# Interleaving the latents' output projection and second norm with the context's layer-1 projections, on split PSUM banks

## The chip, the cores and the metric

The kernel runs on one core of a Trainium2 chip. The metric is the device time of one execution in microseconds (us), median of several runs. The engines are TensorE (PE, matmul), VectorE (DVE), ScalarE (ACT), GpSimd (POOL) and SyncE (SP, which issues most DMAs). PSUM, where matmuls accumulate, is used as eight banks of 128 x 512 fp32 values.

## What is computed

A backbone of two layers reads 512 latent tokens (`lat`) and 256 context tokens (`ctx`), width 1024, both through the same weights. Cut to what matters here, with `x` either stream:

```python
for l in range(DEPTH):                               # DEPTH = 2
    h  = modulate(rmsnorm(x, norm1[l]), ...)         # per-token rms, per-channel scale and shift
    y  = mixers(h @ w_in[l])                         # delta rule, windowed attention, HGRN2
    x  = x + m2 * (y @ w_out[l])                     # output projection, gated residual
    x  = x + m5 * sqrelu_mlp(modulate(rmsnorm(x, norm2[l]), ...), w_ff1[l], w_ff2[l])
return rmsnorm(x_lat, norm_f)
```

The context reads only itself; the latents read context and latents. In the last layer the context is needed only as far as the mixers' keys, values and states, so its layer-1 work is a norm, part of `w_in`, and two recurrences. It has no output projection and no MLP there.

## The kernel before

Activations lie transposed, channels on the 128 partitions, as eight tiles `x[k]` of 128 x T. A product of fp32 precision is made of three matmuls on split operands: high weight times high activation, high times low, low times high (L554, L555 and L556 in `product_t`). `product_t` takes one 128 x 1024 weight piece and makes one 128 x T output in a bank of kind "d": 24 matmuls. `product_n` (L572 to L574) makes the context's or latents' `abvi` outputs token-major, 128 x 400 for each block of 128 tokens (a "cell", two for the context), in banks of kind "dn", over four pieces of two channel tiles each.

Each piece is loaded by SP (L538), rounded to its high half by ACT (the CAST of L540) and its low half is made by DVE (L541). Staging, high and low halves each have a ring of two slots, so a piece's CAST waits until the matmuls of the piece two before it have ended.

A norm has three parts. `rstd` squares the eight tiles on ACT (L627), adds them on DVE (L628), sums over channels with tiny matmuls (L631), takes a Newton inverse root with twelve small DVE instructions (L634, L515 to L520), builds diagonal tiles (L638) and broadcasts the result with a matmul into a bank `pb` (L640). `modulated` then makes, for each of eight tiles, a scaled copy from `pb` (DVE L650), its high half (ACT L653) and its low half (DVE L654). The squares, the scaled copies, the spilled gates and the MLP's temporaries all take their 128 x 512 buffers from one ring of two, `ev`.

PSUM banks are handed out by kind, round robin: "d" has banks 0 and 1, "dn" 0, 1, 3, 4, 5 and 6, "n" 4 to 7.

The order on each engine comes from a scheduler that places the instructions by priority, which is the order in which the Python code emits them; weight pieces are emitted at a raised priority. `run` emits several generators side by side: each yields an estimated number of us, and the one that is furthest behind, after division by its speed, goes next.

Around the change the program is: the context's layer-0 output projection and MLP end; `project(1, (ctx,))` makes the context's layer-1 norm; `out_proj(0, lat)` runs eight products `m0` to `m7` of 512 columns, each evacuated by L1472 onto `x[m]`; the first step of `mlp(0, lat)` makes the latents' norm; `context_in` runs the context's layer-1 projections (`abvi`, then the delta keys and values `k0`, `k1`, `v0`, `v1` with a convolution after each, then the gates `hf00` to `hf11`, whose results are spilled to DRAM by POOL, then `sk`); then the latents' MLP (`ff1`, `ff2`) runs with the context's recurrences beside it.

Of the kernel before, what the change touches and what calls it, by code (L numbers as in the profile page):

```python
# [273 lines left out]
def run(*streams):  # L274

    at = [[0.0, i, g, speed] for i, (g, speed) in enumerate((x if isinstance(x, tuple) else (x, 1.0)) for x in streams)]
    while at:
        a = min(at)
        try:
            a[0] += next(a[2]) / a[3]  # L280
        except StopIteration:
            at.remove(a)
# [22 lines left out]
class Net:  # L305
# [334 lines left out]
        nc.tensor.matmul(pb, lhsT=self.c["ones"], rhs=dg, start=True, stop=True)  # L640
        return pb

    def modulated(self, l, which, seg, pb=None):
        nc = self.nc
        if pb is None:
            pb = self.rstd(seg)
        h = self.split(seg)
        for k in range(8):
            t = self.ev(seg.T)
            nc.vector.scalar_tensor_tensor(out=t, in0=seg.x[k], scalar=self.gmul[l][:, which, k, seg.idx:seg.idx + 1], in1=pb,  # L650
                                           op0=ALU.mult, op1=ALU.mult)
            sh = self.mod(l, 3 * which, k, seg)
            nc.scalar.activation(out=h.hi(k), in_=t, func=AF.Identity, bias=sh)  # L653
            nc.vector.scalar_tensor_tensor(out=h.lo(k), in0=t, scalar=sh, in1=h.hi(k).bitcast(F32), op0=ALU.add, op1=ALU.subtract)  # L654
        return h


    def in_piece(self, l, name):
# [27 lines left out]
    def project(self, l, segs):  # L686

        for seg in segs:
            if seg.x is None:
                self.x_load(seg)  # L690
        pbs = [self.rstd(seg, "n") for seg in segs]
        if l == 0:
            ring = Ring(self, 8, 1024)
            run(self.ada(0, 0, ring))
            ring.free()
        for seg, pb in zip(segs, pbs):
            seg.h = self.modulated(l, 0, seg, pb)
            self.x_free(seg)
            seg.r, seg.b, seg.need = {}, {}, seg is self.lat or l < DEPTH - 1
            if seg is self.ctx:  # L700
                seg.kv0 = l * 256
# [771 lines left out]
            yield from self.product_t(self.io["wout"][l, m][:, ks[0] * 128:(ks[-1] + 1) * 128], [(seg, h)], evac, len(ks))  # L1473
        h.free()

    def mlp(self, l, seg):
        nc = self.nc
        h = self.modulated(l, 1, seg)
        yield 0.0
        f = self.split(seg)  # L1480
        for g in range(4):
            for k in range(8):
                def evac(seg, ps):
                    t = self.ev(seg.T)
                    nc.scalar.activation(out=t, in_=ps, func=AF.Relu)  # L1485
                    nc.scalar.activation(out=t, in_=t, func=AF.Square)  # L1486
                    nc.scalar.copy(f.hi(k), t)  # L1487
                    nc.vector.tensor_tensor(out=f.lo(k), in0=t, in1=f.hi(k).bitcast(F32), op=ALU.subtract)  # L1488
                yield from self.product_t(self.io["ff1"][l, g * 8 + k], [(seg, h)], evac)
            for m in range(8):  # L1490
                def evac(seg, ps):
                    nc.vector.scalar_tensor_tensor(out=seg.x[m], in0=ps, scalar=self.mod(l, 5, m, seg), in1=seg.x[m], op0=ALU.mult, op1=ALU.add)  # L1492
                yield from self.product_t(self.io["ff2"][l, g, m], [(seg, f)], evac)
        h.free()
        f.free()
# [16 lines left out]
    def run(self, stop=None):  # L1512
        self.setup()
        lat, ctx = self.lat, self.ctx
# [40 lines left out]
        def context_in():  # L1555
            self.reserve((ctx,), "dk", "dv")
            yield from self.project_dn(1, (ctx,))
            yield from self.project_hg(1, (ctx,))
            yield from self.project_swa(1, (ctx,))
            ctx.h.free()  # L1560
# [12 lines left out]
        self.region_type(F32R, "r2", "r3")  # L1573
        run(bg.rest())
        self.project(1, (ctx,))
        run(self.out_proj(0, lat))
        mlp = self.mlp(0, lat)
        next(mlp)
        run(context_in())
        Ub = self.delta_open((ctx,))  # L1580

        def context():
# [4 lines left out]
            yield from self.hgrn(1, ctx, False)  # L1587

        run(self.ahead(context(), 3000), mlp)
        self.x_store(lat)  # L1590
        self.main = False
# [70 lines left out]
```

## Time and profile before

| | us |
|---|---|
| median of 3 runs | 2117.33 (2115.97 to 2119.23) |
| profiled execution | 2116.83 |
| span of its trace | 2115.0 |
| PE busy in the span | 1977.7 (94%) |
| DVE busy | 1219.3 (58%) |
| ACT busy | 857.6 (41%) |

A busy time is the sum of an engine's instructions in one profiled execution; lines like L554 are lines of the kernel before. The granted clock is the clock of TensorE that the throttle granted, as a share of full speed: 1.00 is 2.4 GHz and 0.50 is 1.2 GHz. Matmul durations overlap, so the distance from start to start tells the rate.

### The profile page before, as it was taken

How to read it: one execution, taken by the hardware profiler on the slowest of the kernel's cores; microseconds unless marked ns; L12 is line 12 of the kernel's file. 1: busy time of each engine (PE TensorE's matmuls, PEld its weight loads, DVE VectorE, ACT ScalarE, POOL GpSimd, SP SyncE). 2: the span in 40 equal slices, each digit the busy share in tenths (PEclk: the TensorE clock that was granted, in tenths of full speed). 3: DMA queues.
4: the chain of work that ended last, by engine and by line, in shares of the span. 5: the costliest groups of instructions: out<-in, count | busy, mean ns of one | idle time of the engine just before them, and what ended most of it. 6: DMA issues, size and time to landing. Idle time of an engine off the chain costs nothing.

```text
span 2115.0 us, 37910 instructions
## 1 busy us (share of the span) xinstructions
PE 1977.7 (94%) x15456; PEld 1620.8 (77%) x15456; DVE 1219.3 (58%) x2737; ACT 857.6 (41%) x1703; POOL 144.2 (7%) x281
## 2 busy tenths in 40 slices
PE   5999998799999999699999998999899979999996
PEld 2787887688899898588888876767678747888885
DVE  4574856666976667577333334666887483333334
ACT  2432353235465564353434242324555234334241
POOL 0001231200000000010000000011200000000000
PEclk9999999799999999899999999999999999999998
DMA  8435342145233243243222235464300222222221
GB/s 336 156 111 165 93 130 77 57 163 188 95 111 106 100 147 111 85 151 105 95 100 94 96 113 187 140 186 154 122 20 2 81 70 91 99 98 92 100 90 70
DMA packets 72445, 242.43 MB, mean 115 GB/s; under 512 B 10192, under 2 KB 12368, under 8 KB 72144
## 3 DMA queue, kind: packets, MB, share of 16 engines
q1 hardware_dynamic: 57456, 197.35, 27.7%
q0 software_dynamic: 11792, 34.14, 5.1%
q10 hardware_dynamic: 3024, 8.53, 1.2%
q8 instruction: 121, 1.98, 0.4%
q14 instruction: 52, 0.43, 0.1%
HBM read 218.21 MB, written 19.14 MB: 112 GB/s over the span
## 4 chain that ended last, share of the span: by engine, by line
PE 78%; DVE 9%; DMA 6%; issue 4%; ACT 2%; POOL 1%; ACTq 0%; DVEq 0%; POOLq 0%
PE psum L554 20%; PE psum L556 19%; PE psum L555 19%; PE psum L590 2%; PE psum L1444 2%; DMA arena<-in_ada 1%; PE psum L1435 1%; PE psum L1382 1%; DVE weights L541 1%; PE psum L1109 1%; PE psum L1067 1%; PE psum L1261 1%; DMA arena<-in_ff 1%; PE psum L1071 1%; DVE arena L1272 1%
## 5 line engine op out<-in xcount | busy, mean ns | idle before, releaser
L554 PE MATMUL psum<-r,weights 128*128 128x512 f32 (+1 forms) x2304 | 830.4, 361 | 11.7 <-ACT arena L725 4.2
L556 PE MATMUL psum<-r,weights 128*128 128x512 f32 (+1 forms) x2304 | 826.6, 360 | 2.1 <-DVE weights L541 2.0
L555 PE MATMUL psum<-r,weights 128*128 128x512 f32 (+1 forms) x2304 | 825.0, 359 | 1.3 <-DVE r L1464 1.0
L540 ACT CAST weights<-arena 128x1024 fp32r<-128x1024 f32 (+3 forms) x295 | 293.3, 995 | 700.1 <-PE psum L555 600.4
L541 DVE TENSOR_TENSOR weights<-arena,weights 128x1024 fp32r<-128x1024 f32 (+3 forms) x295 | 340.5, 1155 | 294.6 <-ACT weights L540 286.4
L554 PEld LDWEIGHTS psum<-r,weights 128*128 128x128 f32 x2304 | 435.9, 189 | 96.1 <-issue 9.6
L556 PEld LDWEIGHTS psum<-r,weights 128*128 128x128 f32 x2304 | 435.8, 189 | 74.2 <-DVE weights L541 6.3
L555 PEld LDWEIGHTS psum<-r,weights 128*128 128x128 f32 x2304 | 435.8, 189 | 70.1 <-issue 3.9
L1492 DVE SCALAR_TENSOR_TENSOR arena<-psum,arena 128x512 f32<-128x512 f32 (+1 forms) x96 | 63.3, 660 | 200.6 <-PE psum L556 200.4
L1488 DVE TENSOR_TENSOR r<-arena,r 128x512 fp32r<-128x512 f32 (+1 forms) x96 | 57.5, 601 | 35.2 <-ACT r L1487 34.8
L653 ACT ACTIVATE r<-arena 128x512 fp32r<-128x512 f32 (+1 forms) x56 | 33.1, 627 | 71.0 <-DVE arena L650 71.0
L590 PE MATMUL psum<-arena 128*32 128x256 f32 x576 | 53.1, 416 | 9.0 <-DMA arena<-in_ada 8.3
L1382 PE MATMUL psum<-r 128*128 128x256 f32 (+1 forms) x256 | 53.6, 320 | 1.7 <-ACT r L1415 1.3
L1486 ACT ACTIVATE arena<-arena 128x512 f32<-128x512 f32 (+1 forms) x96 | 54.0, 564 | 2.4
L1487 ACT CAST r<-arena 128x512 fp32r<-128x512 f32 (+1 forms) x96 | 52.5, 551 | 2.7 <-ACT arena L1428 0.3
L1485 ACT ACTIVATE arena<-psum 128x512 f32<-128x512 f32 (+1 forms) x96 | 50.2, 523 | 0.0
L1472 DVE SCALAR_TENSOR_TENSOR arena<-psum,arena 128x512 f32<-128x512 f32 (+1 forms) x40 | 27.6, 694 | 33.9 <-PE psum L556 33.8
L572 PE MATMUL psum<-weights,r 128*128 128x400 f32 x96 | 35.4, 382 | 10.7 <-DVE arena L650 10.1
L1382 PEld LDWEIGHTS psum<-r 128*128 128x128 f32 x256 | 37.2, 193 | 5.9 <-ACT r L1415 3.2
L590 PE MATMUL psum<-r,arena 128*32 128x256 f32 x192 | 22.8, 491 | 19.0 <-DMA r<-in_ada 19.0
L1402 DVE TENSOR_REDUCE arena<-psum 128x2 f32<-128x512 f32 x40 | 27.5, 687 | 22.2 <-PE psum L1382 18.0
L627 ACT ACTIVATE arena<-arena 128x512 f32<-128x512 f32 (+1 forms) x56 | 30.7, 549 | 22.8 <-DVE arena L1492 11.9
(426 smaller groups left out, 2576.4 us busy)
## 6 DMA issues: line engine op xcount, KB each, us to landing
arena<-in_ff SPq DMA_DIRECT2D x192, 512.0 KB, 3.2
arena<-in_ada SPq DMA_DIRECT2D x72, 512.0 KB, 4.8
arena<-in_win SPq DMA_DIRECT2D x51, 512.0 KB, 4.0
r<-in_ada SPq DMA_DIRECT2D x24, 512.0 KB, 5.2
arena<-in_wout SPq DMA_DIRECT2D x16, 512.0 KB, 3.3
arena<-in_win SPq DMA_DIRECT2D x12, 400.0 KB, 3.6
arena<-in_x ACTq DMA_DIRECT2D x8, 512.0 KB, 7.0
arena<-arena POOLq DMA_DIRECT2D x40, 64.0 KB, 4.6
```

Source lines behind the costliest of these rows:

```text
L540: nc.scalar.copy(hi, st)
L541: nc.vector.tensor_tensor(out=lo, in0=st, in1=hi.bitcast(F32), op=ALU.subtract)
L554: nc.tensor.matmul(o, lhsT=hi[:, w], rhs=h.hi(k), start=k == 0, stop=False)
L555: nc.tensor.matmul(o, lhsT=hi[:, w], rhs=h.lo(k), start=False, stop=False)
L556: nc.tensor.matmul(o, lhsT=lo[:, w], rhs=h.hi(k), start=False, stop=k == nk - 1)
L590: nc.tensor.matmul(ps[32 * j:32 * j + 32, f * 256:f * 256 + 256], lhsT=self.csil[:, k, :], rhs=st[:, j * 256:j * 256 + 256], start=k == 0, ...
L1382: nc.tensor.matmul(o, lhsT=qs[:, kv], rhs=ks[:, kv, a, c0:c1], start=a == 0, stop=a == 1 and not more)
L1485: nc.scalar.activation(out=t, in_=ps, func=AF.Relu)
L1486: nc.scalar.activation(out=t, in_=t, func=AF.Square)
L1487: nc.scalar.copy(f.hi(k), t)
L1488: nc.vector.tensor_tensor(out=f.lo(k), in0=t, in1=f.hi(k).bitcast(F32), op=ALU.subtract)
L1492: nc.vector.scalar_tensor_tensor(out=seg.x[m], in0=ps, scalar=self.mod(l, 5, m, seg), in1=seg.x[m], op0=ALU.mult, op1=ALU.add)
```

## The change

`modulated` becomes a generator, `modulated_steps`, which yields 6.0 after `rstd` and 1.4 after each of the eight tiles, takes the kind of bank for `rstd`, and has its own ring of two for the scaled copies in place of `ev`; the old `modulated` runs it to the end, so every norm of the kernel gets that ring. `mlp` can be given a finished norm. In `run`, the latents' output projection and norm form one generator, which is emitted side by side with `context_in` at speed 0.5; during this stretch "dn" has banks 3 and 4, "n" 5 and 6, and the latents' `rstd` uses "n". The same operations are issued before and after.

```diff
--- before.py
+++ after.py
@@ -640,19 +640,30 @@
         nc.tensor.matmul(pb, lhsT=self.c["ones"], rhs=dg, start=True, stop=True)
         return pb
 
-    def modulated(self, l, which, seg, pb=None):
+    def modulated_steps(self, l, which, seg, pb=None, bk="d"):
         nc = self.nc
         if pb is None:
-            pb = self.rstd(seg)
-        h = self.split(seg)
+            pb = self.rstd(seg, bk)
+            yield 6.0
+        h, own = self.split(seg), Ring(self, 2, seg.T)
         for k in range(8):
-            t = self.ev(seg.T)
+            t = own()
             nc.vector.scalar_tensor_tensor(out=t, in0=seg.x[k], scalar=self.gmul[l][:, which, k, seg.idx:seg.idx + 1], in1=pb,
                                            op0=ALU.mult, op1=ALU.mult)
             sh = self.mod(l, 3 * which, k, seg)
             nc.scalar.activation(out=h.hi(k), in_=t, func=AF.Identity, bias=sh)
             nc.vector.scalar_tensor_tensor(out=h.lo(k), in0=t, scalar=sh, in1=h.hi(k).bitcast(F32), op0=ALU.add, op1=ALU.subtract)
+            yield 1.4
+        own.free()
         return h
+
+    def modulated(self, l, which, seg, pb=None):
+        g = self.modulated_steps(l, which, seg, pb)
+        while True:
+            try:
+                next(g)
+            except StopIteration as e:
+                return e.value
 
 
     def in_piece(self, l, name):
@@ -1473,10 +1484,11 @@
             yield from self.product_t(self.io["wout"][l, m][:, ks[0] * 128:(ks[-1] + 1) * 128], [(seg, h)], evac, len(ks))
         h.free()
 
-    def mlp(self, l, seg):
+    def mlp(self, l, seg, h=None):
         nc = self.nc
-        h = self.modulated(l, 1, seg)
-        yield 0.0
+        if h is None:
+            h = self.modulated(l, 1, seg)
+            yield 0.0
         f = self.split(seg)
         for g in range(4):
             for k in range(8):
@@ -1573,10 +1585,15 @@
         self.region_type(F32R, "r2", "r3")
         run(bg.rest())
         self.project(1, (ctx,))
-        run(self.out_proj(0, lat))
-        mlp = self.mlp(0, lat)
-        next(mlp)
-        run(context_in())
+
+        def latents():
+            yield from self.out_proj(0, lat)
+            lat.h = yield from self.modulated_steps(0, 1, lat, bk="n")
+
+        self.banks = dict(self.BANKS, dn=(3, 4), n=(5, 6))
+        run(latents(), (context_in(), 0.5))
+        self.banks = self.BANKS
+        mlp = self.mlp(0, lat, lat.h)
         Ub = self.delta_open((ctx,))
 
         def context():
```

Later lines have moved: L650, L653, L654 are L651, L654, L655 in the changed kernel, and L1472 is L1483; L756 evacuates a gate (L745 before), L969, L932, L975, L1002 and L1007 belong to the context's delta preparation. In the rows below a `psum` is any bank, `weights` a half of a weight piece, `arena` and `r` activations; x2 means that the row stands twice.

TensorE, at the end of `m0` (L554 to L556), with the context's column sums (L631). Before:

```order
L555 MATMUL psum<-r_128,weights 128x512
L556 MATMUL psum<-r_128,weights 128x512
L631 MATMUL psum<-arena 128x1 x2
L554 MATMUL psum<-r_7903,weights 128x512
L555 MATMUL psum<-r_7903,weights 128x512
```

and with the change:

```order
L555 MATMUL psum<-r_7903,weights 128x512
L556 MATMUL psum<-r_7903,weights 128x512
L631 MATMUL psum<-arena 128x1 x2
L640 MATMUL psum<-arena 128x256
L572 MATMUL psum<-weights,r_128 128x400
L573 MATMUL psum<-weights,r_128 128x400
```

Before, `m1` follows the column sums; now the broadcast (L640) and the first `abvi` piece do, and `m1` comes after two such pieces.

ScalarE, at the latents' squares (L627). Before, from the last of the output projection to the modulation (L653):

```order
L540 CAST weights<-arena 128x1024
L627 ACTIVATE arena<-arena 128x512 x3
L540 CAST weights<-arena 128x1024
L627 ACTIVATE arena<-arena 128x512
L540 CAST weights<-arena 128x800
L627 ACTIVATE arena<-arena 128x512
L540 CAST weights<-arena 128x800
L627 ACTIVATE arena<-arena 128x512
L653 ACTIVATE r_128<-arena 128x512 x4
L653 ACTIVATE r_7903<-arena 128x512 x4
```

With the change, from the evacuation of `hf00` (first L756) to the modulation (L654):

```order
L540 CAST weights<-arena 128x1024 x2
L756 ACTIVATE arena<-psum 128x256
L969 ACTIVATE arena<-psum 128x4x64
L540 CAST weights<-arena 128x1024
L627 ACTIVATE arena<-arena 128x512
L540 CAST weights<-arena 128x1024
L627 ACTIVATE arena<-arena 128x512 x4
L756 ACTIVATE arena<-psum 128x256
L540 CAST weights<-arena 128x1024
L756 ACTIVATE arena<-psum 128x256 x2
L654 ACTIVATE r_128<-arena 128x512 x2
```

The last five squares now stand behind the evacuation of a context gate and behind CASTs of pieces of the context's projections; the other three gates are evacuated after the squares.

VectorE, at the latents' modulation (first the end of the inverse root, then the diagonal tiles L638). Before:

```order
L520 SCALAR_TENSOR_TENSOR arena<-arena 128x4
L638 TENSOR_SCALAR arena<-arena 128x128 x4
L650 SCALAR_TENSOR_TENSOR arena<-arena,psum 128x512 x2
L654 SCALAR_TENSOR_TENSOR r_128<-arena,r_128 128x512 x2
L650 SCALAR_TENSOR_TENSOR arena<-arena,psum 128x512 x2
```

With the change:

```order
L520 SCALAR_TENSOR_TENSOR arena<-arena 128x4
L638 TENSOR_SCALAR arena<-arena 128x128 x4
L932 COPY arena<-psum 64x16 x4
L1002 TENSOR_TENSOR arena<-arena 128x512 x2
L651 SCALAR_TENSOR_TENSOR arena<-arena,psum 128x512 x2
L541 TENSOR_TENSOR weights<-arena,weights 128x1024
L975 TENSOR_TENSOR arena<-psum,arena 128x256
L655 SCALAR_TENSOR_TENSOR r_128<-arena,r_128 128x512 x2
L651 SCALAR_TENSOR_TENSOR arena<-arena,psum 128x512 x2
L541 TENSOR_TENSOR weights<-arena,weights 128x1024
L1007 TENSOR_TENSOR arena<-arena 128x256
L655 SCALAR_TENSOR_TENSOR r_128<-arena,r_128 128x512 x2
```

Weight splits (L541) and steps of the context's delta preparation now stand between the modulation's instructions. With the change, TensorE's order from there is `m7`, `hf00`, `hf01`, `hf10`, the latents' column sums, `hf11`, the broadcast, `sk`, and the first two `ff1` products tile by tile in turn. The order also differs in two other ways: in the opening, the modulations of the two streams now alternate; and in stretches around 350 to 900 us and 1310 to 1720 us instructions swap places with near neighbours.

## Rows read from the trace of the kernel before

**Rows 1.** The page: busy time of the engines, and the chain by engine.

```profile
PE 1977.7 (94%) x15456; PEld 1620.8 (77%) x15456; DVE 1219.3 (58%) x2737; ACT 857.6 (41%) x1703; POOL 144.2 (7%) x281
...
PE 78%; DVE 9%; DMA 6%; issue 4%; ACT 2%; POOL 1%; ACTq 0%; DVEq 0%; POOLq 0%
```

**Rows 2.** Windows of 25 us: length, busy time per engine, granted clock, DMA.

```profile
850.00:875.00 25.00, 12.23 (x47) 9.28 (x46) 17.21 (x37) 7.13 (x11) 0.53 (x1) 0.75 0.11 33
875.00:900.00 25.00, 20.70 (x142) 19.85 (x141) 13.54 (x32) 12.35 (x21) 1.20 (x3) 0.91 0.42 138
900.00:925.00 25.00, 23.95 (x188) 22.14 (x187) 18.89 (x50) 11.58 (x23) 3.54 (x9) 1.00 0.52 171
```

**Rows 3.** Waits of PE from 780 to 935 us: total, times, longest.

```profile
PE psum L572 <- DVE arena L650: 10.1, 1, 10.1
PE psum L554 <- ACT arena L725: 4.2, 1, 4.2
PE psum L631 <- DVE arena L628: 2.3, 1, 2.3
```

**Rows 4.** Timeline of DVE, 814 to 838 us: start, duration, line; context norm.

```profile
814.80 0.75 DVE L1472 SCALAR_TENSOR_TENSOR arena<-psum,arena 128x512 f32<-128x512 f32 x1 [2.38 <-PE psum L556]
...
817.48 0.16 DVE L634 TENSOR_SCALAR arena<-psum 128x2 f32<-128x2 f32 x1 [0.56 <-PE psum L631]
...
819.65 0.16 DVE L520 SCALAR_TENSOR_TENSOR arena<-arena 128x2 f32<-128x2 f32 x1
...
821.02 0.47 DVE L638 TENSOR_SCALAR arena<-arena 128x128 f32<-128x128 f32 x2
...
826.59 0.87 DVE L650 SCALAR_TENSOR_TENSOR arena<-arena,psum 128x256 f32<-128x256 f32 x2
```

**Rows 5.** Timeline of DVE, 852 to 877 us: the latents' norm.

```profile
854.21 0.75 DVE L1472 SCALAR_TENSOR_TENSOR arena<-psum,arena 128x512 f32<-128x512 f32 x1 [3.32 <-PE psum L556]
...
857.61 0.16 DVE L634 TENSOR_SCALAR arena<-psum 128x4 f32<-128x4 f32 x1 [1.15 <-PE psum L631]
...
862.97 1.41 DVE L650 SCALAR_TENSOR_TENSOR arena<-arena,psum 128x512 f32<-128x512 f32 x2 [1.89 <-PE psum L640]
...
873.15 1.41 DVE L654 SCALAR_TENSOR_TENSOR r<-arena,r 128x512 fp32r<-128x512 f32 x2 [0.19 <-ACT r L653]
```

**Rows 6.** Timeline of PE, 855 to 893 us: start, duration, line.

```profile
856.52 1.05 PE L631 MATMUL psum<-arena 128*128 128x1 f32 x8 [2.34 <-DVE arena L628]
...
858.53 0.34 PE L572 MATMUL psum<-weights,r 128*128 128x400 f32 x1
858.71 0.34 PE L573 MATMUL psum<-weights,r 128*128 128x400 f32 x1
...
860.03 0.54 PE L572 MATMUL psum<-weights,r 128*128 128x400 f32 x1
860.37 0.54 PE L573 MATMUL psum<-weights,r 128*128 128x400 f32 x1
...
861.13 1.80 PE L640 MATMUL psum<-arena 128*128 128x512 f32 x2
```

**Rows 7.** Groups by line and shape, 800 to 925 us: busy, mean ns, idle before.

```profile
L541 DVE TENSOR_TENSOR weights<-arena,weights 128x1024 fp32r<-128x1024 f32 x21 | 25.7, 1222 | 13.5 <-ACT weights L540 13.0
L540 ACT CAST weights<-arena 128x1024 fp32r<-128x1024 f32 x20 | 21.0, 1050 | 37.0 <-PE psum L555 23.9 <-DMA arena<-in_ff 5.3 <-DMA arena<-in_win 5.2
...
L628 DVE TENSOR_TENSOR arena<-arena 128x512 f32<-128x512 f32 x7 | 4.8, 685 | 0.2
```

**Rows 8.** DMA issues, 880 to 925 us: KB each, median us to landing.

```profile
hf_ctx<-arena POOLq DMA_DIRECT2D x4, 128.0 KB, 2.0
```

**Rows 9.** Waits of all engines, 850 to 900 us: total, times, longest.

```profile
ACT arena L930 <- PE psum L929: 2.6, 1, 2.6
```

**Rows 10.** Window of the opening, columns as in Rows 2.

```profile
50.00:75.00 25.00, 21.83 (x129) 18.82 (x127) 16.48 (x27) 8.81 (x14) 0.00 (x0) 0.93 0.52 169
```

**Rows 11.** Timeline of DVE, 44 to 66 us: the opening.

```profile
64.56 0.99 DVE L541 TENSOR_TENSOR weights<-arena,weights 128x800 fp32r<-128x800 f32 x1 [3.48 <-ACT weights L540]
```

## The prediction

> **What bounds the kernel now.** I read the page first: TensorE is busy for 94% of the span, and 78% of the chain that ended last is TensorE's own [rows 1]. Time can only come from stretches in which it waits or runs slowly. The windows show that the stretch of the change holds one: of 75 us from 850 on, PE is busy 12.23, 20.70 and 23.95 of each 25 us, so it is idle for 12.8 + 4.3 + 1.05 = 18.1 us, and the granted clock is 0.75 and 0.91 in the first two [rows 2]. Before 850 and after 925 it hardly idles.
>
> The waits say what ends these gaps: 10.1 us until the last scaled copy of the latents' norm (L650), 4.2 us until an evacuation of `abvi`, 2.3 us until the last squares were added [rows 3]. The 10.1 us are a wait for a bank: `pb`, which L650 reads, lies in a bank that "dn" also hands to the second cell of `abvi`. Behind the idle time the clock is at half speed (1.2 GHz): after the column sums the `abvi` matmuls start 0.18 us apart, and from 859 on 0.33 us apart [rows 6]. By that spacing six matmuls before 861 and nine after 873 lost 0.15 us each; some sixteen of 256 columns after 886 lost about 0.09 us each. That is 0.9 + 1.4 + 1.5 = 3.8 us. So the latents' norm costs **21.9 us** now, 1.0% of the time. It is the ceiling of the gain here.
>
> The context's norm costs nothing: its inverse root, diagonal and scaled copies run on DVE at 817.5 to 836 us, while TensorE runs `m1` to `m4` [rows 4].
>
> **What the change moves: the context's norm.** It puts `abvi` between `m0` and `m1`. The weight rings hold two pieces; `m1` can get its weights only when the first `abvi` piece is done, and TensorE takes its queue in order, so nothing is left to run under the context's norm. Taking `m0` to end at 815.0 (now 814.8), the chain is:
> - column sums on PE 0.5 (two blocks, half of the 1.05 for four [rows 6]), to 815.5;
> - DVE first evacuates `m0` (0.75) and splits the second `abvi` piece (about 1.0), to 816.8; the root takes 2.3 (817.48 to 819.81), the diagonal 0.47 [rows 4], to 819.6. PE is idle for 4.1 us;
> - the broadcast: 1.80 us for two passes of 512 columns at half clock [rows 6]; for 256 columns I take 0.6, to 820.2;
> - the first high half is there after a scaled copy (0.87 for two [rows 4]) and one step of ACT, about 1.1 us;
> - 24 `abvi` matmuls, 4.4 us at 0.18 us apart, run at 0.33 us for the first 3 us or so after the gap: 1.8 us more;
> - `m1`'s piece: CAST 1.05 and split 1.22 [rows 7] begin when the first `abvi` piece ends, some 2 us before the second does: 0.8 us of wait.
>
> The sum is 4.1 + 1.1 + 1.8 + 0.8 = **7.8 us of new loss**. Its ends are 5 us, if the clock stays high and the weights are not late, and 11 us, if all runs at half clock up to `m1`.
>
> **The latents' norm.** From `m1` to `m7` work is dense: products of the context stand between those of the latents, so the loads and casts have cover. Call T the end of `m7`. Behind it stand `hf00`, `hf01`, `hf10`, 2.8 us each: half of a 512-column product, of which seven took 854.21 - 814.80 = 39.4 us [rows 4, 5]. They cover 8.5 us. The column sums need the last squares, and these are late for a reason of the change: they stand on ACT behind CASTs that wait for TensorE, and in the ring `ev` behind a spill. In us after T: `hf00` ends at 2.8; a CAST (1.05) and the evacuation (0.4) follow, and the spill's DMA is issued at about 4.3; it takes 2.0 us or more to land [rows 8], so the slot is free near 6.9. A square and two additions (0.69 each [rows 7]) end at 8.9. The next CAST waits for the end of `hf10`, 8.5, and ends at 9.6; DVE's split of it at 10.8; the last four additions at 13.6. **PE is idle for 5.1 us**, between 2 us (the spill lands at once and the CAST is early) and 8 us (spill 2.5 us later).
>
> Then: column sums 1.05, to 14.7; `hf11` 2.8 and 1.6 more at half clock, to 19.1, while DVE makes root and diagonal (3.9 us for the latents, 857.61 to the broadcast [rows 5, 6]); the broadcast 1.8 (as now), to 20.9; `sk` to 23.7. From 20.9 DVE modulates: four pairs of tiles at 2.9 us (862.97 to 874.56 [rows 5]) are 11.6 us, two splits between them 2.4, and some six steps of the context's delta preparation 3.2: the last half is ready at 38.1. The two `ff1` products, tile by tile behind it, need 11.2 us and small matmuls between them 3.5; they would end at 38.4 undisturbed, and end at 39.5: 1.1 us lost. Both weight slots are then held to the end, so CAST and split of the next piece stand open: 2.0 us. After T the loss is 5.1 + 1.6 + 1.1 + 2.0 = **9.8 us**.
>
> What is gained here is 21.9 - 7.8 - 9.8 = **4.3 us**, with ends of -3 and +9 from the ends of the terms.
>
> The split of banks by itself removes the 10.1 us wait [rows 3]; in the sum it stands inside the 21.9. Before, the stretch is one of DVE: from 850 to 875 it is busy 17.21 of 25 us and PE 12.23, while the projections around it keep PE busy 23.95 of 25 [rows 2]. The Trainium skill, page "Perfetto Trace Analysis", section "Optimization Strategy", says that where the most contended engine changes over time, interleaving the two regimes may help. By that alone the sum would be the first rival's below, 2101; by the queues, which the chains above follow, it is 4.3 us of gain here, and I take the queues, as each of their waits has a named releaser.
>
> **The opening.** All norms get a ring of their own, and in the opening the two streams' modulations alternate. There PE is idle for 3.2 of 25 us [rows 10], and DVE waits 3.48 us, in the midst of the modulation, for a weight CAST that waited for TensorE [rows 11]. The norm should end earlier, but TensorE's work there stays and its clock dips. Between 0 and 3.2 us I take **1.5 us**, the middle. At the two later norms of the latents alone nothing uses `ev` beside them: nothing.
>
> **Reshuffled stretches.** The scheduler's small swaps at 350 to 900 and 1310 to 1720 us have no known sign. I take 0, with 4 us to either side: less than half of what a single lost cover costs (10.1).
>
> The sum is 4.3 + 1.5 + 0 = 5.8 us: 2116.83 - 5.8 = 2111.0. The profiled execution lies 0.5 us under the median, so I forecast **2111.5** for the median.
>
> **Rivals.** *The gap closes* (chance 0.10): the context's norm finds cover, or its 7.8 us shrink to 3, and the latents' last squares come before `hf10` ends, so the 5.1 us go. The gain is 5.8 + 4.8 + 5.1 = 15.7: about 2101. For it: DVE and ACT are far from full in the stretch [rows 2]. Against it: each of these waits follows from a queue's order, and a queue waits however idle its engine is.
>
> *The bubble only moves* (0.29): one bubble of 21.9 becomes two of which each has its wait, its half clock and its restart of the weights. If the first costs 9.5 instead of 7.8, the second 11.5 instead of 9.8, and the opening gives nothing, the gain is 0.9: about 2116.5. For it: the clock fell within 3 us of the gap's start [rows 6], so each new gap pays again.
>
> *Ping-pong in the modulation* (0.18): slower. Four steps of the delta preparation on DVE (two L975, two L1007) now stand between the latents' scaled copies and need a result of TensorE, which itself stands behind `ff1` matmuls that wait for those copies. Each such crossing could add a wait that the sum doesn't have: 1.15 us for DVE behind the column sums [rows 5], 2.6 us for ACT behind a small matmul [rows 9]. At 2.6 us four cost 10.4: about 2122. It ends slower than before from 1.5 us a crossing on, and measurably so from 2.5. Against it: before, the modulation shows no such waits, but it ran alone.
>
> **How the numbers follow.** A measurement of this kernel can tell about 0.2% from no change, 4.2 us: below 2113.1 is faster, above 2121.5 slower. The forecast's own case (2106 to 2113) has 0.43, the gap that closes 0.10: faster 0.53. The bubble that moves has 0.29, ping-pong and unlucky swaps 0.18. The range reaches from 2101 (the closed gap) to 2122 (ping-pong at its full price).
>
> **What would show it.** In the changed profile: PE idle for some 4 us behind `m0`, released by the diagonal (L638), with the clock at 0.5 behind it; no wait of `abvi` for a scaled copy of the latents; `m7`'s evacuation near 885 instead of 854; some 5 us of idle PE ahead of the latents' column sums, released by an addition (L628); the second `ff1` product ending near T + 40. An idle stretch much shorter than 4 us at `m0`, or none at the latents' squares, speaks for the closed gap; waits of L975 or L1007 for PE in the modulation, above 2 us each, for ping-pong. The forecast is wrong in its ground if PE's idle time between 810 and 935 us has not changed by 2 to 12 us, or if other stretches move by more than 4.

## The result and the profile after

| | before | after |
|---|---|---|
| median, us | 2116.51 (7 runs) | 2127.05 (2125.0 to 2136.18, 7 runs) |
| ratio to before | | 1.0053 [1.0042, 1.0065] |
| profiled execution | 2116.83 | 2127.48 |
| span of its trace | 2115.0 | 2125.7 |

The change makes the kernel 0.5% slower, about 11 us; 2111.5 was forecast, with 2122 as the upper end. The page of after shows the same instructions and nearly the same busy times as [rows 1]. Only TensorE's share of the chain has fallen from 78 to 76%, and "issue" has risen from 4 to 7%:

```profile
PE 1978.7 (93%) x15456; PEld 1625.6 (76%) x15456; DVE 1216.0 (57%) x2737; ACT 856.5 (40%) x1703; POOL 144.1 (7%) x281
...
PE 76%; DVE 9%; issue 7%; DMA 5%; ACT 2%; POOL 1%; ACTq 0%; DVEq 0%; POOLq 0%; SPq 0%
```

The windows (columns as in [rows 2]) show that the stretch of the change was not where the time went. PE's idle time from 850 to 925 us is 6.0 us against 18.1 before, though 4.7 us now lie between 800 and 825, where the context's norm stands alone. In the opening PE is busy 24.55 us of the window of [rows 10], against 21.83:

```profile
50.00:75.00 25.00, 24.55 (x152) 20.73 (x151) 16.14 (x31) 10.72 (x20) 0.55 (x1) 1.00 0.58 202
800.00:825.00 25.00, 20.27 (x136) 17.59 (x134) 19.08 (x40) 11.03 (x18) 1.10 (x2) 0.96 0.42 134
825.00:850.00 25.00, 23.89 (x106) 20.80 (x106) 14.77 (x27) 10.18 (x18) 0.00 (x0) 0.91 0.28 90
850.00:875.00 25.00, 25.00 (x149) 22.06 (x148) 15.63 (x32) 13.10 (x22) 1.50 (x6) 1.00 0.41 136
875.00:900.00 25.00, 22.25 (x144) 20.10 (x142) 18.25 (x41) 9.74 (x15) 1.59 (x3) 1.00 0.40 145
900.00:925.00 25.00, 21.72 (x124) 18.31 (x125) 21.19 (x48) 11.81 (x23) 2.69 (x5) 0.86 0.30 101
```

To find where the loss lies I use the **lag**: the difference between the times at which after and before have done the same matmul work, read where their orders of instructions have met again; negative is ahead of before. It is −4.8 us at 300 us, +4.7 at 800, −0.4 at 975 and +11.1 at 1750. So after gains 4.8 in the opening, **loses 9.5 from 300 to 800**, gains 5.1 in the stretch of the change, and **loses 11.5 from 975 to 1750**. Both losses lie where the prediction had "reshuffled stretches, 0". A lag is read from one execution. Where a kernel has the order of before, it still changed by up to 2.4 us from the start to 300 us (e11) and by 3.0 us from 1305 to 1446 us (e11 again); and five kernels with one and the same order on TensorE from 300 to 800 us (e3, e4, e5, e7 and e9) spread from −0.7 to +3.4 there. I take 4 us as its uncertainty.

The second loss can be read without a lag, between the column sums (L631) of the latents' layer-1 norm and those of their second norm. I call this part the tail. The timeline of PE (start, duration, line) shows the two ends, before:

```profile
1305.22 1.05 PE L631 MATMUL psum<-arena 128*128 128x1 f32 x8 [1.36 <-DVE arena L628]
...
1724.65 1.05 PE L631 MATMUL psum<-arena 128*128 128x1 f32 x8 [3.18 <-DVE arena L628]
```

and after:

```profile
1304.63 1.05 PE L631 MATMUL psum<-arena 128*128 128x1 f32 x8 [1.36 <-DVE arena L628]
...
1734.87 1.87 PE L631 MATMUL psum<-arena 128*128 128x1 f32 x8 [3.30 <-DVE arena L628]
```

That is 419.4 us before and 430.2 after, with the same work between.

### The profile page after: what moved, and what is told of

Read it like the earlier page. It is cut to its first block, busy times and chain, and to the rows that moved or that the text cites. A ratio compares the mean times of both kernels' runs of the same rounds, so it can differ in the third digit from the quotient of the medians.

```text
span 2125.7 us, 37874 instructions
## 1 busy us (share of the span) xinstructions
PE 1978.7 (93%) x15456; PEld 1625.6 (76%) x15456; DVE 1216.0 (57%) x2737; ACT 856.5 (40%) x1703; POOL 144.1 (7%) x281
## 4 chain that ended last, share of the span: by engine, by line
PE 76%; DVE 9%; issue 7%; DMA 5%; ACT 2%; POOL 1%; ACTq 0%; DVEq 0%; POOLq 0%; SPq 0%
PE psum L554 20%; PE psum L556 19%; PE psum L555 19%; PE psum L590 2%; PE psum L1455 1%; PE psum L1446 1%; PE psum L1393 1%; DMA arena<-in_ada 1%; DVE weights L541 1%; PE psum L1120 1%; PE psum L1078 1%; PE psum L1272 1%; PE psum L1082 1%; DVE arena L1276 1%; DMA arena<-in_wout 1%
## 5 line engine op out<-in xcount | busy, mean ns | idle before, releaser
L554 PE MATMUL psum<-r,weights 128*128 128x512 f32 (+1 forms) x2304 | 831.7, 362 | 12.8 <-DVE arena L1483 3.1
L556 PE MATMUL psum<-r,weights 128*128 128x512 f32 (+1 forms) x2304 | 828.4, 360 | 2.5 <-DVE weights L541 2.4
L554 PEld LDWEIGHTS psum<-r,weights 128*128 128x128 f32 x2304 | 436.8, 190 | 97.3 <-issue 12.7
L541 DVE TENSOR_TENSOR weights<-arena,weights 128x1024 fp32r<-128x1024 f32 (+3 forms) x295 | 340.7, 1156 | 293.1 <-ACT weights L540 284.7
L556 PEld LDWEIGHTS psum<-r,weights 128*128 128x128 f32 x2304 | 436.3, 189 | 76.5 <-DVE weights L541 6.7
L1498 ACT ACTIVATE arena<-arena 128x512 f32<-128x512 f32 (+1 forms) x96 | 54.0, 564 | 2.4
L1451 ACT COPY arena<-psum 128x512 f32<-128x512 f32 x72 | 41.2, 588 | 28.6 <-PE psum L1446 27.7
L1455 PE MATMUL psum<-arena 128*64 128x128 f32 x640 | 47.4, 287 | 3.8 <-ACT arena L1439 3.7
L1483 DVE SCALAR_TENSOR_TENSOR arena<-psum,arena 128x512 f32<-128x512 f32 (+1 forms) x40 | 27.7, 696 | 37.6 <-PE psum L556 34.2
L1455 PEld LDWEIGHTS psum<-arena 128*64 128x64 f32 x640 | 36.0, 141 | 10.1 <-ACT arena L1439 4.6
L654 ACT ACTIVATE r<-arena 128x512 fp32r<-128x512 f32 (+1 forms) x40 | 23.6, 633 | 42.7 <-DVE arena L651 42.7
```

The source lines that it names most:

```text
L541: nc.vector.tensor_tensor(out=lo, in0=st, in1=hi.bitcast(F32), op=ALU.subtract)
L554: nc.tensor.matmul(o, lhsT=hi[:, w], rhs=h.hi(k), start=k == 0, stop=False)
L556: nc.tensor.matmul(o, lhsT=lo[:, w], rhs=h.hi(k), start=False, stop=k == nk - 1)
L1455: nc.tensor.matmul(py[heads[kv]], lhsT=self.vS[:, blocks[k0 + kt], heads[kv]], rhs=PT[:, c:c + 128], start=k0 + kt == 0, stop=k0 + kt == n ...
```

## The experiments

All are compared with before in runs on the same chip. Where a kernel has more lines, its numbers differ from those of before; the text gives the old one. The medians come from several chips, on which before has medians of 2116.3 to 2119.0 us, so the ratios compare with each other and the medians do not. The last columns are the lag at the end of each part less that at its start, from the profiled execution. That execution lies above the kernel's median by 11.6 us in e2, 7.5 in e4, 5.9 in e6 and 4.8 in e11, so where a single us matters I go by the ratio.

| kernel | median, us | ratio [95%] | 300 to 800 | stretch | tail |
|---|---|---|---|---|---|
| after | 2127.05 | 1.0053 [1.0042, 1.0065] | +9.5 | −5.1 | +11.5 |
| e1 own ring alone | 2131.38 | 1.0064 [1.0039, 1.0089] | +7.1 | +0.4 | +11.2 |
| e2 after, without the ring | 2125.72 | 1.0035 [1.0019, 1.005] | +0.3 | −1.5 | +19.8 |
| e3 e1, ages kept | 2118.72 | 0.9999 [0.9982, 1.0016] | +0.6 | −0.5 | +4.8 |
| e4 after, ages kept | 2121.8 | 1.0032 [1.001, 1.0054] | +3.4 | −0.8 | +12.3 |
| e5 after, at the places of before | 2124.91 | 1.0032 [1.0018, 1.0046] | +2.6 | −4.2 | +10.4 |
| e6 e5, other order | 2121.15 | 1.0016 [1.0004, 1.0029] | +9.0 | −4.1 | +9.3 |
| e7 only the norm beside | 2112.79 | 0.998 [0.9961, 1.0] | −0.7 | −12.1 | +9.4 |
| e8 an unused ring | 2133.77 | 1.0077 [1.0061, 1.0092] | +9.7 | +1.9 | +7.8 |
| e9 e7 at speed 2 | 2113.9 | 0.9987 [0.9978, 0.9997] | −0.7 | −11.9 | +9.2 |
| e10 banks alone | 2124.7 | 1.0039 [1.0025, 1.0052] | +0.6 | −1.9 | +11.2 |
| e11 one priority in layer 1 | 2119.54 | 1.0019 [1.0005, 1.0034] | −0.4 | −0.7 | +6.7 |
| e12 one speed in layer 1 | 2121.55 | 1.0027 [1.0015, 1.0038] | +0.9 | −0.7 | +7.2 |

**Own ring or interleaving (e1, e2).** The diff has two parts that can be told apart: the ring of two in every norm, and the interleaving with its banks. e1 has only the ring:

```diff
-        h = self.split(seg)
+        h, own = self.split(seg), Ring(self, 2, seg.T)
         for k in range(8):
-            t = self.ev(seg.T)
+            t = own()
 ...
+        own.free()
```

> The kernel before, with the norm's own ring of two as the only change; no interleaving, banks as before. Theory A (the own ring is freed after each norm, which shifts the ages by which all later buffers are placed, and with them the order in 350 to 800 us): the same order as the changed kernel up to 800 us, so 4.7 us ahead of before at 300 us and 4 to 5 us behind at 800 us; then PE's idle 18 us at 850 to 925 as before. In all about before plus 5 us, up to 12 more or less from 1300 to 1750 us. Rival B (the losses come from the interleaving and the banks): ahead by 4.7 at 300 us and still at 800 us, about 2112 in all.

e2 is after with `t = self.ev(seg.T)` and without the ring.

> The changed kernel with the scaled copies back in the shared ring ev: interleaving and banks alone. Theory A: level with before up to 800 us, then 4 to 6 us ahead at 975 us; what 1300 to 1750 us do is open (if the loss of 11 us there belongs to the interleaving, about 2122; if it belongs to the own ring, about 2112). Rival B: 9 us behind at 800 us already.

The ring alone costs what the whole change costs, 1.0064, and takes its loss from 300 to 800 with it. Without the ring that loss is gone (+0.3), and so is the opening's gain: e2 has the order of before up to 800 us, and its lag of +2.3 at 300 us only shows how far two executions of one order differ. The interleaving is worth 1.5 us instead of the 4 to 6 that were expected. But the tail loses in both, and both have another instruction order there.

**Why a ring of two 128 x 512 buffers costs time (e3, e4, e8).** A buffer gets its place by age: the allocator (`find`) prefers blocks that were freed long ago, counted in frees, so that a new buffer seldom waits for the last reader of an old one. A ring that is freed after each norm counts as two more frees and leaves two young blocks, and later buffers go elsewhere. Another place means other instructions to wait for, and so, I supposed, another order from the scheduler. e3 (e1) and e4 (after) put the count and the ages back as they were when the ring is freed:

```diff
+        old = Mem.clock, [(m, list(m.t)) for m in [self.mem] + [m for _, m in self.region.values()]]
+        own = Ring(self, 2, seg.T)
 ...
-        own.free()
+        own.forget(old)
```

> The kernel before with the norm's own ring, whose buffers get back the ages that they had before the norm, so that later buffers are placed as before; no interleaving. Theory A: 4.7 us ahead at 300 us and still 4 to 5 us ahead at 800 and at 1300 us; with 1300 to 1750 us as before, about 2112. Rival C (the earlier end of the opening itself upsets 350 to 800 us): about 9 us lost there as in the changed kernel, 4 to 5 us behind at 800 us.

> The changed kernel, its own ring with ages kept. Theory A: 4 to 5 us ahead at 800 us, 9 to 10 us ahead at 975 us; 1300 to 1750 us open: with the changed kernel's loss of 11 us there about 2118, without it about 2107. Rival C: 4 to 5 us behind at 800 us, level at 975 us.

e8 is before with a ring that nothing uses:

```diff
         h = self.split(seg)
+        unused = Ring(self, 2, seg.T)
         for k in range(8):
 ...
+        unused.free()
```

> The kernel before, where each norm takes a ring of two and frees it again without using it: nothing changes but the ages by which later buffers are placed. Theory A or D: as the own ring alone from 350 us on, that is 7 to 9 us lost from 350 to 800 us and 5 to 15 from 1300 to 1750 us, about 2130. If it costs nothing, the own ring's use is what costs, by the changed waits.

These show where the loss from 300 to 800 comes from. A ring that no instruction touches costs 1.0077, and from 300 to 800 as much as after (+9.7). With the ages kept the ring costs nothing: e3 is at 0.9999, and on TensorE the order from 300 to 800 is that of before but for one swap near 505 us. e4 loses less than after, but still 1.0032. Both gain less than was expected: the opening gives 1.6 and 1.8 us with the ages kept, not 4.7, and e4's stretch 0.8, not 5.

**Addresses or order (e5, e6).** Is it the new addresses themselves, or the order that follows from them? In e5 a table puts every buffer at its place of before; the own ring stands only in the opening and in the latents' second norm of layer 0, with ages kept, and the bank counters are set back after the stretch, so that banks too come round as before.

```diff
+        planned = place([self.mem] + [m for _, m in self.region.values()], words)
+        if planned:
+            return planned
 ...
-        h, own = self.split(seg), Ring(self, 2, seg.T)
+        own = self.own_ring(seg) if bk == "n" or pb is not None and l == 0 else None
 ...
-            t = own()
+            t = own() if own else self.ev(seg.T)
 ...
+            own.forget(old)
 ...
+        self.bank_i["n"] -= 2
+        self.bank_i["d"] += 2
```

> The changed kernel, but every buffer lies where it lies in the kernel before (a table of places), the banks' turns are set back after the stretch, and the own ring is used in the opening and in the interleaved norm alone, with ages kept. The scheduler's order still differs from before from 1500 us on by itself. Theory D (the places of the buffers cost the time): about 1 to 2 us ahead at 800 us, 2 to 6 us ahead at 975 us, and no loss from 1300 to 1750 us: about 2112. Rival E (any other order of the scheduler costs there, with the same places): 5 to 12 us lost from 1500 to 1750 us, about 2120.

e6 is e5 with `own.free()`: the same places, but not the same ages, hence other places for the rings of the opening only.

> As the run with the places of before, but the own rings of the opening lie apart, as in the changed kernel. From 100 to 800 us the buffers lie as in the kernel before and the scheduler's order differs. Theory D: 3 to 5 us ahead at 300 us and still at 800 us. Rival E: 5 to 10 us are lost between 350 and 800 us, as in the changed kernel.

Outside the opening and the stretch both have all addresses of before. e5 also has its order from 300 to 800, but for the swap near 505 us, and loses 2.6 there, within the uncertainty; e6 has another order, and loses 9.0. In the tail no instruction of either has another address than before, and they lose 10.4 and 9.3. So it is the **order**, not the address. e6's profiled execution lies well above its median; by the ratio the kernel is 3.4 us slower in all, with some 8 us gained in the opening and the stretch, so its two losses together are nearer to 11 than to 18 us. e5 shows the gain of the stretch clear of the first loss: −4.2.

**Is the tail's order of before special (e11, e12)?** These leave all of before as it is and change one number that acts in layer 1 only: a priority (e11), or the speed of one stream beside another (e12). Their order differs from before only from about 1460 and about 1310 us on.

```diff
-        run(self.ahead(delta(), 3000), self.ahead(att(), 1000), hg())
+        run(self.ahead(delta(), 3000), self.ahead(att(), 1100), hg())
```

> The kernel before with one number changed, the lead that layer 1's attention gets in the order (1000 to 1100). Same instructions, same places; the order differs from about 1460 us on and nowhere before. Rival E (another order of the scheduler costs there, whatever made it): level to 1450 us, 3 to 12 us lost by 1750 us, about 2120 to 2129. Rival F (the changes to the norm leave something behind that costs there): within 2 us of before.

```diff
-        run(self.project_dn(1, (lat,)), ada(1, 1))
+        run(self.project_dn(1, (lat,)), (ada(1, 1), 0.9))
```

> The kernel before with one number changed, the speed of the modulation's weight stream beside layer 1's first projections (1.0 to 0.9). Same instructions; the order differs from about 1310 us on and nowhere before. Rival E: 3 to 12 us lost by 1750 us, about 2120 to 2129. Rival F: within 2 us of before.

Both are slower than before, by 1.0019 and 1.0027, which is 4 and 6 us, with the same instructions at the same places. e11 was not level up to 1450 us, as was expected: 3.0 of its 6.7 us arise between 1305 and 1446, where its order is still that of before. In all, 13 kernels have an order of the tail other than that of before (12 orders: e6 and e9 have the same one on TensorE), and every one loses there in its profiled execution (4.8 to 19.8 us; e3's 4.8 is not seen in its ratio, and e2's 19.8 come from an execution 11.6 us above its median). Before was profiled once, and a lucky execution of it would look like a loss in all 13. The ratios, over many executions, speak against that: e11 and e12, which differ in the tail alone, are slower, and e7 and e9 below, 14 us ahead at 1300 us, end only 4.2 and 2.8 us faster. The order of before is a favourable one, and an edit that disturbs it has to expect a loss.

**What the stretch could give (e7, e9, e10).** e7 runs the whole output projection first and only the norm beside `context_in`, on split banks, with everything else at the places of before.

```diff
-        run(latents(), (context_in(), 0.5))
+        run(self.out_proj(0, lat))
+
+        def norm():
+            lat.h = yield from self.modulated_steps(0, 1, lat, bk="n")
+
+        run(norm(), (context_in(), 0.5))
```

> As the run with the places of before, but the whole output projection comes first, and only the latents' norm runs beside the context's projections: m1 to m4 cover the context's norm again, and the abvi and k products the latents' norm. By the sum's own terms (no wait for L638, none for L628) the stretch should then lose 2 to 6 us instead of 21.9: 14 to 19 us ahead at 975 us in all, with 1 to 2 of it from the opening. From 1300 to 1750 us as the other runs: 2100 without a loss there, about 2110 with one.

e9 is e7 with 2.0 for 0.5.

> As the norm beside the projections, with the context's stream at speed 2.0: of the orders built, the one whose order from 1300 to 1750 us differs least from the kernel before (on TensorE only around 1300 us and from about 1480 to 1580 us). Opening 1 to 2 us ahead, level to 800 us, 12 us gained by 975 us as in the run before it. Theory (another order of the scheduler costs there): at most half of the 7 to 12 us that the other orders lost from 1300 to 1750 us, so 2102 to 2108. If the loss comes whatever the order, about 2112 again.

Here the context's norm keeps the cover of `m1` to `m4`, and the latents' norm has the context's projections as cover. Both of after's new waits are gone. The waits of PE in e7 from 810 to 960 us (total, times, longest) have one of size left: the delta preparation (L957 in before) for the convolution (L680 in before):

```profile
PE psum L1037 <- DVE arena L760: 6.3, 1, 6.3
```

In the windows of e7 this is most of the 6.7 us of idle PE between 875 and 900, with DVE busy 24.82 of 25 us:

```profile
850.00:875.00 25.00, 22.46 (x144) 20.84 (x143) 15.69 (x37) 14.94 (x24) 1.63 (x3) 1.00 0.44 146
875.00:900.00 25.00, 18.31 (x143) 17.65 (x142) 24.82 (x64) 11.56 (x21) 2.56 (x8) 0.86 0.34 122
900.00:925.00 25.00, 25.00 (x144) 20.85 (x144) 18.96 (x46) 15.87 (x29) 1.63 (x3) 1.00 0.39 132
```

The stretch gains 12.1 us of the 21.9 that the prediction gave as its ceiling. Although the tail still loses 9.4, e7 is faster than before, 0.998 [0.9961, 1.0], and e9 more surely so, 0.9987 [0.9978, 0.9997]. e9's order in the tail differs from that of before in few places, on TensorE at 1325 to 1338, 1528 to 1591 and 1696 to 1700 us of before. It loses 9.2 all the same, where at most half of 7 to 12 was expected. But it loses them in those places, as the starts of the same instructions in both timelines show (lines of before):

| | before, us | e9, us | e9 less before |
|---|---|---|---|
| column sums, L631 | 1305.22 | 1291.07 | −14.15 |
| copy, L594 | 1361.47 | 1350.50 | −10.97 |
| copy, L1043 | 1524.58 | 1513.78 | −10.80 |
| copy, L1290 | 1606.50 | 1600.14 | −6.36 |
| reduction, L1177 | 1682.56 | 1676.21 | −6.35 |
| column sums, L631 | 1724.65 | 1719.29 | −5.36 |

Where the orders are the same, from 1361 to 1525 and from 1606 to 1683 us, the difference stays within 0.2 us; where they differ, e9 falls back by 3.2, 4.4 and 1.0.

e10 splits the banks in before and does nothing else:

```diff
+        self.banks = dict(self.BANKS, dn=(3, 4), n=(5, 6))
         run(context_in())
+        self.banks = self.BANKS
```

> The kernel before, with nothing but the banks split for the context's projections (dn 3 and 4, n 5 and 6); the norm is still issued ahead of them, in the shared ring. If the shared bank is what held TensorE for 10.1 us, abvi and k products run under the latents' modulation: 8 to 14 us ahead at 975 us. If the norm's place in the order is what held it, 0 to 4 us. From 1300 to 1750 us its order differs from before from about 1480 us on: 5 to 12 us lost by the theory, about 2110 to 2116 in all.

The 10.1 us of [rows 3] are gone: `abvi` and the keys run during the modulation. But the same wait as in e7 stands in their place, and is longer; here too DVE does the modulation and the convolutions at once (waits of PE, 810 to 960 us):

```profile
PE psum L957 <- DVE arena L680: 8.7, 2, 8.2
```

So the banks alone are worth 1.9 us, which is within the uncertainty, where 8 to 14 were expected if the bank was what held TensorE. The norm needs other work on TensorE and room on DVE, and a bank only gives the first.

## Why the prediction was wrong

**The stretch of the change: right in its mechanism.** PE's idle time from 810 to 935 us, for which a change of 2 to 12 us was forecast, falls by 5.4 (the first window is before, the second after). The longest waits of PE in after, from 790 to 960 us, are three that the chains named; the rest are 1.1 us and less. The prediction had 5.1, 4.1 and 1.1 us:

```profile
810.00:935.00 125.00, 106.88 (x591) 91.93 (x590) 85.53 (x192) 55.45 (x93) 6.91 (x16) 0.93 0.32 105
...
810.00:935.00 125.00, 112.25 (x636) 96.02 (x635) 87.05 (x188) 57.38 (x98) 6.50 (x15) 0.95 0.33 110
...
PE psum L631 <- DVE arena L628: 5.5, 1, 5.5
PE psum L640 <- DVE arena L638: 4.2, 1, 4.2
PE psum L572 <- ACT r L654: 1.1, 1, 1.1
```

The evacuations of `m0` and `m7` and the last additions, from the timeline of DVE, stand where the chains put them once the 4.4 us by which the kernel is already late at 810 us are counted: `m7` is evacuated at 888.55, 4.4 before that is 884.15, and 885 was forecast. The squares are added and the column sums start 14.2 us after it (902.75, the last line, from PE's timeline), where 13.6 was forecast:

```profile
819.60 0.75 DVE L1483 SCALAR_TENSOR_TENSOR arena<-psum,arena 128x512 f32<-128x512 f32 x1 [3.25 <-PE psum L556]
...
823.52 0.48 DVE L638 TENSOR_SCALAR arena<-arena 128x128 f32<-128x128 f32 x2
...
888.55 0.75 DVE L1483 SCALAR_TENSOR_TENSOR arena<-psum,arena 128x512 f32<-128x512 f32 x1
...
899.63 3.07 DVE L628 TENSOR_TENSOR arena<-arena 128x512 f32<-128x512 f32 x4
...
902.75 1.86 PE L631 MATMUL psum<-arena 128*128 128x1 f32 x8 [5.50 <-DVE arena L628]
```

PE's timeline shows the context's broadcast and first `abvi` matmuls at half clock: they start 0.33 us apart, as after the gap in [rows 6]. The broadcast takes 1.22 us, where the prediction took 0.6:

```profile
824.06 1.22 PE L640 MATMUL psum<-arena 128*128 128x256 f32 x2 [4.16 <-DVE arena L638]
826.39 0.70 PE L572 MATMUL psum<-weights,r 128*128 128x400 f32 x1 [1.11 <-ACT r L654]
...
827.23 0.54 PE L572 MATMUL psum<-weights,r 128*128 128x400 f32 x1
827.56 0.54 PE L573 MATMUL psum<-weights,r 128*128 128x400 f32 x1
```

The second `ff1` product is evacuated at 932.60, 44 us after `m7`, where 40 was forecast, and at 932.70 in before (timelines of ACT, after and before):

```profile
932.60 0.59 ACT L1497 ACTIVATE arena<-psum 128x512 f32<-128x512 f32 x1
...
932.70 0.59 ACT L1485 ACTIVATE arena<-psum 128x512 f32<-128x512 f32 x1
```

The 4 us more are not a wait: PE is busy 18.33 of the 19 us from 914 to 933, and the context's small matmuls between the two products, for which 3.5 us were allowed, have busy times of 7.4 us in sum. With the lag of 4.4 taken off, 4.5 us are gained at this point. By the lag over the whole stretch it is 5.1, in e5 4.2 and in e6 4.1. The forecast was **4.3**, and one bubble of 21.9 us did become two smaller ones. That the number was met so closely is in part luck. e2 and e4, interleaved in the same way, gain only 1.5 and 0.8: both have the two long waits (5.7 and 4.2 us), and e4 another of 2.6 us behind the evacuation of a product on ACT.

One reading of [rows 6] was wrong, and decided nothing: the clock did not fall within 3 us of the gap's start. PE was idle from 854.2 to 856.5 us, and at 858.5 the matmuls still started 0.18 us apart.

**The opening: perhaps too low.** 1.5 us were taken, from 0 to 3.2; the profiled execution shows 4.8. The ring alone gives 3.1 in e1, which has after's order in the opening, and 1.6 in e3. With 4 us of uncertainty neither the middle nor the bound is refuted.

**The reshuffled stretches: the step that failed.** The prediction took "0, with 4 us to either side" for the swaps at 350 to 900 and 1310 to 1720 us. They cost 9.5 and 11.5. Two things were wrong in it. The sign was held to be open, but all 13 kernels with another order of the tail lost there. And the size was taken as less than half of one lost cover (10.1 us), whereas the swaps touch two stretches of 400 to 500 us with waits in many places. With 9.5 + 11.5 in place of 0, the prediction's own sum gives 2116.83 − 4.3 − 1.5 + 21.0 = 2132.0; with the opening as measured it is 2128.7, against 2127.48 in the profiled execution.

What such an order looks like in the trace: the windows (columns as in [rows 2]) from 375 to 520 us and from 300 to 800 us, first before, then after, show PE busy 6.7 us less in the 500 us, with 94 matmuls fewer done, and in the shorter stretch a clock of 0.88 in place of 0.92:

```profile
375.00:520.00 145.00, 133.43 (x2108) 115.03 (x2109) 90.41 (x234) 57.09 (x114) 16.93 (x23) 0.92 0.42 137
300.00:800.00 500.00, 470.60 (x5640) 421.88 (x5639) 342.48 (x841) 247.33 (x574) 28.97 (x47) 0.95 0.34 114
```

```profile
375.00:520.00 145.00, 132.84 (x1993) 114.14 (x1992) 81.51 (x219) 52.09 (x106) 8.30 (x14) 0.88 0.37 117
300.00:800.00 500.00, 463.90 (x5546) 418.25 (x5545) 333.11 (x826) 241.00 (x561) 28.85 (x47) 0.95 0.34 113
```

From 375 to 520 us the waits of PE add up to 12.1 us in both; they have moved. Before, PE waits 5.4 us once behind the delta rule's norm (L1181), and 1.3 us in all for the queries of the HGRN scan (L1272), in the order total, times, longest:

```profile
PE psum L1189 <- DVE arena L1181: 5.4, 1, 5.4
...
PE psum L1261 <- DVE arena L1272: 1.3, 2, 0.9
```

After, the scan's matmul (now L1272, for L1283) waits seven times:

```profile
PE psum L1272 <- DVE arena L1283: 8.0, 7, 2.8
```

e6 and e8, as slow there, wait elsewhere: 3.8 and 7.4 us for a DMA (`xu_lat`) at L1067 of before, where before waits 0.9. In the tail after's loss is spread over several waits of 2 to 5 us (waits of PE, 1480 to 1760 us):

```profile
PE psum L1272 <- DVE r L1283: 5.0, 2, 2.6
PE psum L1200 <- DVE r L1192: 3.8, 1, 3.8
PE psum L1455 <- ACT arena L1439: 3.7, 1, 3.7
```

and over windows like these, in which PE does 3 us less, before:

```profile
1525.00:1550.00 25.00, 23.70 (x294) 18.86 (x292) 16.67 (x50) 14.61 (x47) 10.89 (x15) 0.94 0.27 85
...
1575.00:1600.00 25.00, 22.20 (x444) 19.06 (x438) 24.50 (x59) 7.57 (x23) 0.00 (x0) 0.93 0.01 2
```

after:

```profile
1525.00:1550.00 25.00, 20.57 (x268) 16.16 (x265) 16.94 (x61) 15.01 (x51) 10.09 (x15) 1.00 0.30 96
...
1575.00:1600.00 25.00, 19.00 (x380) 17.03 (x382) 24.64 (x51) 8.32 (x24) 0.00 (x0) 0.93 0.01 2
```

The waits differ from order to order, and it **stays open** what in an order makes it slower. That the order decides and not the address is shown by e6 from 300 to 800 us, and in the tail by e5, e6, e7 and e9 to e12, in which no matmul of the tail has another address than before; that the ring changes the order through the ages of the allocator, by e3 and e8. By which dependencies it goes on from there was not followed: e6 has the addresses of before from the opening on and yet another order, and the tail's order changes without the ring too (e2, e10).

**The rivals.** The side was slower, to which 0.18 was given, but not by the named mechanism. Ping-pong did not come about: from 905 to 935 us DVE waits for TensorE twice, 1.1 and 0.8 us, and neither is at L975 or L1007. The gap did not close; the bubble moved, and at a gain. The last sentence of the prediction was the right one: other stretches moved by more than 4.

## What to carry to other kernels

Where a list scheduler or an allocator by age sets the order, ask first what an edit does to stretches that it does not touch: here an unused ring of buffers cost 16 us (1.0077), three times what the rebuilt stretch gave in after. Compare the orders over the whole kernel, hold them fast where the edit has no business (places, ages, banks), and give an order that is lost a price and a sign, not zero. When a norm stalls TensorE, leave those norms that have cover where they are, and bring other work only to the one that has none (e7).

## What the runs showed of the hardware

The same idle time can cost a different clock. In the profiled execution of e10's tail PE is idle for 29.5 us, in before's for 29.8, and yet it takes 429.8 us instead of 419.4. The difference is work at 1.2 GHz, 45.5 us of PE's busy time against 23.5: the 22 us more, at half speed, cost about 11. All 13 other tails have more such work than before, 28.2 to 51.2 us, and ten of them more idle time too (up to 41.2 us in after); so both are part of what those orders cost, each read from one execution. In one window, first e10 and then before, nearly the same busy share of PE goes with a granted clock of 0.69 and 0.93:

```profile
1550.00:1575.00 25.00, 24.05 (x383) 20.72 (x382) 19.66 (x38) 9.18 (x24) 0.00 (x0) 0.69 0.05 17
```

```profile
1550.00:1575.00 25.00, 24.44 (x450) 21.39 (x450) 23.07 (x51) 12.78 (x35) 0.00 (x0) 0.93 0.04 13
```

Which gaps bring the clock down was not tried apart. Idle time alone, which is most of what the prediction summed, does not price an order.
